# Gathers that fill a bank before copying it, earlier weight loads, and the crowded experts' loop at the end of the expert stage

## The chip, the cores and the metric

One core of one Trainium2 chip runs the kernel in a single launch. The metric is device time in microseconds (us), from one run of the program on the chip; the table below gives the median of three runs and the time of one profiled execution. TensorE (PE) does the matmuls, ScalarE (ACT) and VectorE (DVE) work between PSUM and SBUF, GpSimd (POOL) splits and subtracts in SBUF, and SyncE (SP) issues the DMAs. TensorE's clock is granted by the chip at one of two levels, 2.4 or 1.2 GHz; the profile gives the mean of a stretch as a share of full speed.

## The reference

Two layers, each a mixer (attention and a gated convolution, output matrix `wo`), a mixture of 32 experts (MoE) and a per-layer embedding stage (PLE), on 512 tokens of width 1024. The part that the change touches is the MoE:

```python
# x: 512 tokens x 1024; per layer
n      = rms_norm(x) * nf                 # normalised tokens
p      = softmax(n @ router)              # routing weights over the experts
picks  = the experts chosen for a token, weight g
for e in experts:
    rows = tokens that chose e
    h    = silu(n[rows] @ wg[e]) * (n[rows] @ wu[e])
    x[rows] += g[rows, e] * (h @ wdn[e])
```

Each expert has three weight matrices (`wg`, `wu`, `wdn`) of fp32 numbers, which are read from DRAM once per layer.

## The kernel before

**Pairs of experts.** An expert has room for 64 tokens; two experts form a pair, whose 128 rows fill TensorE's output partitions, 64 each. There are 16 pairs a layer and eight rounds `c` of two pairs. The order of a round on TensorE is written out in `moe`: for each of the two pairs the blocks `g` (the `wg` product) and `u` (the `wu` product), with 32 matmuls each; then `y` (64 matmuls, the `wdn` product of the round before); transposes `hT` of the two pairs; the gather `xg` for the next round (64 matmuls); the combine `c` (32 matmuls) of the round before, which VectorE adds into the tokens (L1079). After the eighth round come the last `y`, a last combine and the PLE stage, whose raw chunks pg0 to pg7 `load_chunks` loads.

**The gather.** Tokens are kept as two parts, `xh` (rounded) and `xl` (the rest). A one-hot matrix picks a pair of pairs' 256 rows. The 1024 columns of a token are worked in eighths k; the two eighths 2h and 2h+1 share one PSUM bank of 512 columns, 256 each, and an eighth is 8 matmuls (four token tiles, two parts). `gather(oh, xg, h)` is called for h = 0 to 3. ScalarE copies each eighth to SBUF (L998). The gather for the first round is made in parts while the tokens are routed (L901, copied by L990), and its last part takes the branch `if self.xg0`.

**Other work of ScalarE in a round.** L1034 starts silu on `g`, L1045 copies the transposes, L1065 scales `y` by the routing weight (`yh`), L1110 rounds the embedding matrix pT that `embeddings` uses in rounds 5 and 6.

**Buffers and queues.** All large tiles (weights, tokens, `xh`, `xl`, `xg`, raw chunks of the other matrices and their split halves) come from 45 slots of 128 x 1024 fp32 (`s4`), handed out in a ring. A weight load is half a matrix row block, 512 KB, and one SP instruction (L241 in `pump`; L253 loads eight late halves of 256 KB). `pump(limit, keep)` issues loads in a fixed order as long as slots are free (keeping `keep` of them) and fewer than `limit` are outstanding. SP issues one DMA at a time in program order, so a load whose slot is not yet free, or whose turn among the eight DMA semaphores has not come, holds all behind it. `RING` gives the limits in the mixer's tail: RING[0] in the eight `ao` steps, RING[1] behind them and in the `wo` steps, RING[2] in the hook that runs while the tokens are routed (`route_tile`, four tiles t).

**Crowded experts.** `overflow` handles experts with more than 64 tokens, in a loop whose count comes from the routing. In this data no expert has that many, so the loop body runs zero times. The loop itself (L1217, L1218) is nevertheless entered: every engine, SP included, comes to its start and waits for all engines and for all DMAs issued so far. Before, it stands in round 4 (`if c == OVC`), behind the combine of pairs 6 and 7.

Of the kernel before, what the change touches and what calls it, by code (L numbers as in the profile page):

```python
# [8 lines left out]
F32 = mybir.dt.float32  # L9
# [3 lines left out]
AF = mybir.ActivationFunctionType  # L13
# [4 lines left out]
T, D, P = 512, 1024, 128  # L18
NT = T // P
# [7 lines left out]
CAP = 64  # L27
GS = 256
# [25 lines left out]
              + [f"wo{i}" for i in range(8)] + ["pe0", "pe1"] + [f"pg{i}" for i in range(8)])  # L54
NCH = len(SEQ_CHUNKS)

RING = 2, 12, 20
KEEP = 6, 10, 6, 6, 8, 10, 12, 8
LAGS = 1, 2, 1, 5
OVC = 4  # L60
PEC = 5
PGD = "pg1", "pg2", "pg3"
PGS = 1, 3, 4, 5, 7
# [18 lines left out]
class Pinned:  # L82


    def __init__(self, tc, e):
        self.tc, self.e = tc, e
# [69 lines left out]
class Trunk:  # L156
    def __init__(self, ctx, tc, x, pT, wd, wg, wu, wdn, sm, gains, cst, out):
        self.tc, self.nc = tc, tc.nc
        self.L = wd.shape[0]
        self.dr = dict(x=x, pT=pT, wd=wd, g=wg, u=wu, d=wdn, sm=sm, gains=gains, cst=cst, out=out)  # L160
        one = ctx.enter_context(tc.tile_pool(name="one", bufs=1))
        rot = ctx.enter_context(tc.tile_pool(name="rot", bufs=1))
        pp = ctx.enter_context(tc.tile_pool(name="ps", bufs=8, space=PSUM))
        self.one, self.tiny = one, ctx.enter_context(tc.tile_pool(name="tiny", bufs=1))
        self.s4 = Slots(rot, "s4", 1024, N4)
        self.s2 = Slots(rot, "s2", 512, N2)
        self.ps = Slots(pp, "ps", 512, 8)
        self.x = [self.s4.get(F32, "x") for _ in range(NT)]
        self.c1 = one.tile([P, C_N1], F32, name="c1")
        self.smt = one.tile([P, S_N], F32, name="smt")  # L170
        self.ident = self.c1[:, C_ID:C_ID + P]
        self.raw, self.hl = {}, {}
        self.loaded = self.split_n = 0
        self.queues, self.adv_n = [], 0

        self.items, self.item_tile, self.item_next, self.ring = [], {}, 0, 0
        for l in range(self.L):
            for c in range(NPAIR // 2 + 1):
                for p in (2 * c, 2 * c + 1) if 2 * c < NPAIR else ():
                    self.items += [(l, w, 2 * p + e, h) for w in ("g", "u") for h in range(4) for e in range(2)  # L180
                                   if p or w == "u" or h < 4 - LATE]
                for p in (2 * c - 2, 2 * c - 1) if c else ():
                    self.items += [(l, "d", 2 * p + e, h) for h in range(4) for e in range(2)]
# [283 lines left out]
    def mixer(self, l):  # L467
        nc = self.nc
        v, act = nc.vector, nc.scalar
# [254 lines left out]
        for j in range(8):  # L724
            c = pos[f"ao{j}"]
            wh, wl = self.take(c)
            pab = [self.ps.get(F32, "ya"), self.ps.get(F32, "yb")]
            for s, src in ((1, cv), (0, oT)):
                for k in range(4):
                    w = slice((4 * s + k) * P, (4 * s + k + 1) * P)  # L730
                    self.mm3(pab[s], wh[:, w], wl[:, w], src[0](k), src[1](k), k == 0, k == 3)
            self.done(c)
            g = gates.pop(0)
            ga, gb = g[:, :T], g[:, T:]
            act.activation(pab[1], pab[1], AF.Identity, bias=self.smt[:, S_BO + j:S_BO + j + 1])
            v.scalar_tensor_tensor(gb, gb, 1.0, pab[1], op0=OP.add, op1=OP.mult)
            v.scalar_tensor_tensor(pab[0], ga, 1.0, pab[0], op0=OP.add, op1=OP.mult)
            v.tensor_tensor(pab[0], pab[0], gb, op=OP.add)
            for h in range(2):
                a = slice(256 * h, 256 * h + 256)  # L740
                act.activation(mT[0].half(j, h), pab[0][:, a], AF.Copy, scale=0.5)
                v.scalar_tensor_tensor(mT[1].half(j, h), pab[0][:, a], 0.5, mT[0].half(j, h).bitcast(F32),
                                       op0=OP.mult, op1=OP.subtract)
            self.ps.free(2)
            self.s4.free()
            self.pump(RING[0])
        for s in oT + tuple(cv):
            s.free()
        self.pump(RING[1])

# [15 lines left out]

        def hook():
            self.advance(steps)
            self.pump(RING[2])
        for t in range(NT):  # L770
            steps.append(self.route_tile(t))
            self.half[t] = self.token_b(cs, mT, t, hook)
# [24 lines left out]
    def route_tile(self, t):  # L797

        nc = self.nc
        v, act, pe = nc.vector, nc.scalar, nc.tensor  # L800
        x, r = self.x[t], self.rc[:, t:t + 1]
# [28 lines left out]
            yield  # L830
        transposes(1)

        hi, lo = self.s4.get(F32R, "xh"), self.s4.get(F32R, "xl")
        act.activation(hi, x, AF.Copy)
        nc.gpsimd.tensor_tensor(lo, x, hi.bitcast(F32), op=OP.subtract)
# [14 lines left out]
        w = self.lgw[:, t * P:(t + 1) * P]  # L850
# [114 lines left out]
    def moe(self, l):  # L965
        nc = self.nc
        self.nc = Engines(self.tc, ("te",))
        v, act, pe = nc.vector, nc.scalar, self.nc.tensor
        oh = self.oh0
# [12 lines left out]
        def gather(oh, xg, h):  # L982

            scale = lambda k: self.smt[:, S_NF + k:S_NF + k + 1]
            out = lambda k: xg[h // 2][:, (k % 4) * GS:(k % 4 + 1) * GS]
            if self.xg0:
                for k in (2 * h, 2 * h + 1):
                    ps = self.xg0.pop(0)[:, :GS]
                    self.gather_part(ps, oh, k, NT - 1)
                    self.last_a = act.activation(out(k), ps, AF.Copy, scale=scale(k)).ins  # L990
                    self.ps.free()
                return
            ps = self.ps.get(F32, "xg")
            for i in range(2):
                k, w = 2 * h + i, slice(i * GS, (i + 1) * GS)
                for t in range(NT):
                    self.gather_part(ps[:, w], oh, k, t)
                act.activation(out(k), ps[:, w], AF.Copy, scale=scale(k))  # L998
            self.ps.free()

        oht, gs, rh, hT, ys = {}, {}, {}, {}, {}
# [118 lines left out]
        NC2 = NPAIR // 2  # L1120
# [5 lines left out]
        for c in range(NC2):  # L1126
            self.c = c
            prs = 2 * c, 2 * c + 1
            if c == PEC - 1:
                load_embeddings()  # L1130
            if c < NC2 - 1:
                oh = self.onehots(c + 1)
            ts = []
            for p in prs:
                pg, pu = self.ps.get(F32, "g"), self.ps.get(F32, "u")
                gate_up(p, xg, "g", pg, range(4))
                gate_up(p, xg, "u", pu, range(4))
                if p == 0:
                    with self.tc.issue_after(self.last_v), self.tc.issue_after(self.last_a):
                        self.route()  # L1140
                        make_rows()
                scatter_hot(p)
                ts.append(hidden(p, pg, pu))
            self.s4.free(2)
            if c == 1:
                restore()
            if c:
                for p in prs:
                    down(p - 2)
            for p, t in zip(prs, ts):  # L1150
                transp(p, t)
            if c < NC2 - 1:
                xg = [self.s4.get(F32, "xg") for _ in range(2)]
                for h in range(4):
                    gather(oh, xg, h)
                self.s4.free()
                if c == NC2 - 2:
                    self.s4.free(2 * NT)
            if c:
                combine((2 * c - 2, 2 * c - 1))  # L1160
            if c == OVC:
                self.overflow(l)
            if c in (PEC, PEC + 1):
                embeddings(c - PEC)
# [5 lines left out]
        pe = nc.tensor  # L1170
# [41 lines left out]
    def overflow(self, l):  # L1212
        nc = self.nc
        v, act, pe, ov = nc.vector, nc.scalar, nc.tensor, self.ov
# [3 lines left out]
        with self.tc.For_i(0, n, 1):  # L1218
            was = self.s4.used, self.s2.used, self.ps.used
            fa, fb, fr = self.s4.get(F32, "ova"), self.s4.get(F32, "ovb"), self.s4.get(F32R, "ovr")  # L1220
            sc, xg, hh, hT, oh, oht = fa[:, :T], fa[:, T:], fb[:, :T], fb[:, T:], fr[:, :T], fr[:, T:]
# [39 lines left out]
            ps = self.ps.get(F32, "ooht")  # L1261
# [5 lines left out]
            for i, q in enumerate((vg, self.rc)):  # L1267
                for t in range(NT):
                    pe.matmul(pg[0:CAP, i:i + 1], oh[:, t * CAP:(t + 1) * CAP].bitcast(F32), q[:, t:t + 1],
                              start=t == 0, stop=t == NT - 1)  # L1270
# [2 lines left out]
            v.tensor_scalar(g[0:CAP], g[0:CAP], rr[0:CAP], None, op0=OP.mult)  # L1273
            self.ps.free()
            px = self.ps.get(F32, "oxg")
            for k in range(KD):
                for t in range(NT):
                    for o in range(2):
                        pe.matmul(px[:, k * CAP:(k + 1) * CAP], self.nh[o][t][:, k * P:(k + 1) * P],
                                  oh[:, t * CAP:(t + 1) * CAP], start=t == 0 and o == 0, stop=t == NT - 1 and o == 1)  # L1280
                act.activation(xg[:, k * CAP:(k + 1) * CAP], px[:, k * CAP:(k + 1) * CAP], AF.Copy,
                               scale=self.smt[:, S_NF + k:S_NF + k + 1])
            self.ps.free()
            pgu = []
            for w in ("g", "u"):
                p_ = self.ps.get(F32, "ogu")
                for h in range(4):
                    wt = weights(w, h)
                    for k in range(2):
                        kk = 2 * h + k  # L1290
                        pe.matmul(p_[0:CAP], xg[:, kk * CAP:(kk + 1) * CAP], wt[:, k * T:(k + 1) * T],
                                  start=kk == 0, stop=kk == KD - 1)
# [13 lines left out]
            for f in range(4):  # L1306
                wt = weights("d", f)
                for n_ in range(2):
                    pe.matmul(py[n_][0:CAP], hT[:, f * CAP:(f + 1) * CAP], wt[:, n_ * T:(n_ + 1) * T],
                              start=f == 0, stop=f == 3)  # L1310
# [172 lines left out]
```

## Time and profile before

| | |
|---|---|
| median of 3 runs | 1946.11 us (1943.98 to 1948.0) |
| profiled execution | 1943.51 us |
| its span, first to last instruction | 1941.7 us, so 1.8 us lie around it |
| mean granted TensorE clock | 0.974 of full |
| TensorE busy | 1812.1 us, 93% |
| DVE, ACT, POOL busy | 916.9, 565.8, 377.9 us |
| DMA queue of SP | 477.04 MB, 65.1% of 16 engines' span |
| MoE of layer 0 | first `g` at 399.7 us, last `y` ends at 916.1 |
| MoE of layer 1 | first `g` at 1360.2 us, last `y` ends at 1871.3 |

A row of the timeline is: start, duration, engine, line of the kernel, operation, output <- inputs, shape, count; in brackets the idle time of the engine just before it and what ended it. Matmuls overlap, so the rate is read from their starts, not from their durations. In a table of stretches "(x8)" is the number of instructions that began there, PEclk the granted clock as a share of full, and the last two columns are the DMA engines' busy share and GB/s. "DVEq", "SPq" stand for an engine's sequencer.

### The profile page before, as it was taken

Reading aid. Unit: us, or ns where it says so; the run is one execution under the profiler, and the core shown is the slowest. Engines: PE = TensorE matmul, PEld = TensorE weight load, DVE = VectorE, ACT = ScalarE, POOL = GpSimd, SP = SyncE. Lnnn points to the kernel's source line nnn. Section 1 sums busy time; section 2 is a strip of 40 time slices with the busy share of each in tenths; the row PEclk is TensorE's granted clock in tenths of the full one; section 3 lists DMA queues with packets and bytes.
Section 4 is the critical chain, followed back from the end, with each engine's and each line's share of the span. In section 5 each row is a group of like instructions: output and inputs, shape, how many; then the busy total and the mean of one; then the engine's idle time right before and its main releaser. Section 6 shows DMA issues by size and latency. Waiting matters only on the chain. (4 is left out here: it accounts for less than half of the span.)

```text
span 1941.7 us, 23302 instructions
## 1 busy us (share of the span) xinstructions
PE 1812.1 (93%) x8532; PEld 1124.4 (58%) x8532; DVE 916.9 (47%) x2165; ACT 565.8 (29%) x1071; POOL 377.9 (19%) x201
## 2 busy tenths in 40 slices
PE   5999999999999889999989999998999989999987
PEld 4776777753454345354767776877444553454456
DVE  5677754652431332323657777537432423332146
ACT  4444444220111012112634555333110111021045
POOL 3444324201000000000444444241010000000021
PEclk9999999999989999999999999999999999999999
DMA  5211227589999889997231112375898989899941
GB/s 217 83 55 66 65 98 227 189 321 357 349 351 410 343 312 382 388 409 303 81 117 65 61 59 66 127 242 195 308 401 326 381 351 401 349 364 409 409 176 44
DMA packets 133319, 478.59 MB, mean 246 GB/s; under 512 B 14800, under 2 KB 15312, under 8 KB 133200
## 3 DMA queue, kind: packets, MB, share of 16 engines
q1 hardware_dynamic: 133200, 477.04, 65.1%
q8 instruction: 70, 1.15, 0.2%
q14 instruction: 49, 0.40, 0.1%
HBM read 474.89 MB, written 2.10 MB: 246 GB/s over the span
## 5 line engine op out<-in xcount | busy, mean ns | idle before, releaser
L230 POOL TENSOR_TENSOR s_lo<-s_raw,s_hi 128x1024 fp32r<-128x1024 f32 x114 | 272.3, 2400 | 950.5 <-ACT s_hi L225 326.6
L94 PE MATMUL ps_g<-s_w,s_xg 128*64 128x512 f32 x1024 | 230.9, 604 | 4.4 <-DVEq L1218 4.4
L94 PE MATMUL ps_y<-s_w,s_hT 128*64 128x512 f32 x1024 | 225.8, 593 | 0.4 <-DMA s_w<-wdn 0.4
L94 PE MATMUL ps_u<-s_w,s_xg 128*64 128x512 f32 x1024 | 225.2, 592 | 0.0
L290 PE MATMUL ps_z<-s_hTl,s_hi 128*128 128x512 f32 x512 | 204.4, 399 | 0.0
L289 PE MATMUL ps_z<-s_hTh,s_hi 128*128 128x512 f32 x512 | 202.0, 395 | 0.0
L291 PE MATMUL ps_z<-s_hTh,s_lo 128*128 128x512 f32 x512 | 200.4, 391 | 0.0
L94 PE MATMUL ps_xg<-s_OH,s_xh 128*128 128x256 f32 x476 | 138.9, 322 | 59.6 <-ACT s_xg L998 55.8
L1079 DVE TENSOR_TENSOR s_x<-s_x,ps_c 128x512 f32<-128x512 f32 x128 | 87.9, 687 | 155.6 <-PE ps_c L94 132.4
L94 PEld LDWEIGHTS ps_y<-s_w,s_hT 128*64 128x64 f32 x1024 | 74.5, 137 | 148.4 <-issue 136.2
L94 PEld LDWEIGHTS ps_g<-s_w,s_xg 128*64 128x64 f32 x1024 | 73.0, 139 | 149.7 <-issue 142.2
L94 PEld LDWEIGHTS ps_u<-s_w,s_xg 128*64 128x64 f32 x1024 | 73.4, 137 | 146.3 <-issue 141.2
L501 DVE SCALAR_TENSOR_TENSOR s_acc<-ps_z,smt,s_acc 128x511 f32<-128x511 f32 (+27 forms) x210 | 153.7, 732 | 4.2
L94 PEld LDWEIGHTS ps_xg<-s_OH,s_xh 128*128 128x128 f32 x476 | 101.4, 213 | 74.2 <-ACT s_xg L998 68.5
L94 PE MATMUL ps_xg<-s_OH,s_xl 128*128 128x256 f32 x476 | 130.9, 305 | 0.0
L225 ACT ACTIVATE s_hi<-s_raw 128x1024 fp32r<-128x1024 f32 x120 | 124.5, 1055 | 0.7
L1034 ACT ACTIVATE s_h<-ps_g,rs 128x512 f32<-128x512 f32 x32 | 22.0, 687 | 343.1 <-PE ps_g L94 331.8
L1035 DVE SCALAR_TENSOR_TENSOR s_h<-s_h,ps_g 128x512 f32<-128x512 f32 x32 | 22.0, 687 | 188.2 <-ACT s_h L1034 188.2
L290 PEld LDWEIGHTS ps_z<-s_hTl,s_hi 128*128 128x128 f32 x512 | 96.7, 189 | 21.4 <-issue 3.0
L289 PEld LDWEIGHTS ps_z<-s_hTh,s_hi 128*128 128x128 f32 x512 | 96.5, 189 | 21.5 <-issue 1.0
L291 PEld LDWEIGHTS ps_z<-s_hTh,s_lo 128*128 128x128 f32 x512 | 96.5, 189 | 19.1
L1045 ACT ACTIVATE s_hT<-ps_hT 128x512 f32<-128x512 f32 x32 | 17.6, 596 | 304.1 <-PE ps_hT L94 263.2
(256 smaller groups left out, 2873.9 us busy)
## 6 DMA issues: line engine op xcount, KB each, us to landing
s_w<-wu SPq DMA_DIRECT2D x256, 512.0 KB, 10.1
s_w<-wdn SPq DMA_DIRECT2D x256, 512.0 KB, 10.2
s_w<-wg SPq DMA_DIRECT2D x248, 512.0 KB, 10.2
s_raw<-wd SPq DMA_DIRECT2D x124, 512.0 KB, 3.5
s_w<-wg SPq DMA_DIRECT2D x16, 256.0 KB, 7.9
s_x<-x SPq DMA_DIRECT2D x4, 512.0 KB, 9.4
out<-s_n SPq DMA_DIRECT2D x8, 256.0 KB, 2.0
s_gain<-gains SPq DMA_DIRECT2D x3, 512.0 KB, 3.7
```

The costliest lines, as they stand in the source:

```text
L94: i = f(*a, **k)
L225: nc.scalar.activation(hi, raw, AF.Copy)
L230: nc.gpsimd.tensor_tensor(lo, raw, hi.bitcast(F32), op=OP.subtract)
L289: mm(out, lh, rh, start=start, stop=False)
L290: mm(out, lh, rl, start=False, stop=False)
L291: mm(out, ll, rh, start=False, stop=stop)
L501: v.scalar_tensor_tensor(o, i, w, o, op0=OP.mult, op1=OP.add)
L1034: act.activation(t, pg, AF.Tanh, scale=rh[p])
L1035: v.scalar_tensor_tensor(t, t, 1.0, pg, op0=OP.add, op1=OP.mult)
L1045: act.activation(o, ps, AF.Copy)
L1079: v.tensor_add(xs, xs, ps)
```

## The change

Five things. `gather` writes both eighths of a bank and only then issues the two copies. `RING` goes from 2, 12, 20 to 6, 18, 28, its first limit grows by one in each `ao` step, and the last pump keeps three slots free. `route_tile` writes each token tile x[t] to a DRAM scratch `xk` before splitting it. The loop of the crowded experts moves from round 4 to the end of round 7, behind the combine of pairs 12 and 13 and ahead of the last `y`. Its body, which runs zero times here, reads the tokens from the scratch.

```diff
-RING = 2, 12, 20
+RING = 6, 18, 28
-OVC = 4
...
-            self.pump(RING[0])
+            self.pump(RING[0] + j)
...
-            self.pump(RING[2])
+            self.pump(RING[2], keep=3)
...
+        if t == 0:
+            self.xkept = [self.dram.tile([P, D], F32, name=f"xk{i}", tag=f"xk{i}") for i in range(NT)]
+        self.nc.sync.dma_start(self.xkept[t], x)
         hi, lo = self.s4.get(F32R, "xh"), self.s4.get(F32R, "xl")
...
             ps = self.ps.get(F32, "xg")
+            half = [ps[:, i * GS:(i + 1) * GS] for i in range(2)]
             for i in range(2):
-                k, w = 2 * h + i, slice(i * GS, (i + 1) * GS)
                 for t in range(NT):
-                    self.gather_part(ps[:, w], oh, k, t)
-                act.activation(out(k), ps[:, w], AF.Copy, scale=scale(k))
+                    self.gather_part(half[i], oh, 2 * h + i, t)
+            for i in range(2):
+                act.activation(out(2 * h + i), half[i], AF.Copy, scale=scale(2 * h + i))
             self.ps.free()
...
-            if c == OVC:
+            if c == NC2 - 1:
                 self.overflow(l)
...
+            xt = []
+            for t in range(NT):
+                xt.append(self.s4.get(F32, "ox"))
+                nc.sync.dma_start(xt[t], self.xkept[t])
```

TensorE's matmuls in the rounds keep their order. On ScalarE, the place is the gather at the end of round 3 (`ps_xg` are its four banks, `pTh` the rounded embedding matrix, L1110 before and L1114 after). Before:

```order
L998 ACTIVATE s_xg_4685<-ps_xg_4687,smt 128x256 x2
L998 ACTIVATE s_xg_4685<-ps_xg_4706,smt 128x256 x2
L998 ACTIVATE s_xg_4686<-ps_xg_4725,smt 128x256 x2
L998 ACTIVATE s_xg_4686<-ps_xg_4744,smt 128x256
L1110 ACTIVATE s_pTh_4811<-s_pT_4813 128x1024
L998 ACTIVATE s_xg_4686<-ps_xg_4744,smt 128x256
```

And after:

```order
L1002 ACTIVATE s_xg_4695<-ps_xg_4697,smt 128x256 x2
L1002 ACTIVATE s_xg_4695<-ps_xg_4716,smt 128x256 x2
L1002 ACTIVATE s_xg_4696<-ps_xg_4735,smt 128x256 x2
L1002 ACTIVATE s_xg_4696<-ps_xg_4754,smt 128x256 x2
L1114 ACTIVATE s_pTh_4821<-s_pT_4823 128x1024
```

The last eighth's copy stood behind the embedding matrix and now stands ahead of it.

On SP, the place is the loop of layer 0 (the branches). Before, round 4, with weight loads on both sides:

```order
L241 DMA s_w_5054<-wu 128x1024
L241 DMA s_w_5060<-wg 128x1024
L241 DMA s_w_5062<-wg 128x1024
L1218 COMPARE_AND_BRANCH
L1218 UNCONDITIONAL_BRANCH x2
```

After, behind the last weight of the layer, with the PLE stage's raw chunks following:

```order
L241 DMA s_w_6292<-wdn 128x1024
L241 DMA s_w_6298<-wdn 128x1024
L1222 COMPARE_AND_BRANCH
L1222 UNCONDITIONAL_BRANCH x2
L1486 BRANCH_PREFETCH_HINT
L1283 DMA s_ox_6475<-xk_2813 128x1024
L1283 DMA s_ox_6477<-xk_2814 128x1024
L1283 DMA s_ox_6479<-xk_2815 128x1024
L1283 DMA s_ox_6481<-xk_2816 128x1024
L1222 REGISTER_ALU
L1222 COMPARE_AND_BRANCH
```

The four scratch reads lie inside the loop. SP comes to the loop with no weight of the layer left to issue.

Also on SP, the end of the mixer of layer 0 after the change, where the fourth token tile (`x_72`) is written to the scratch:

```order
L241 DMA s_w_3105<-wg 128x1024
L241 DMA s_w_3107<-wg 128x1024
L241 DMA s_w_3109<-wg 128x1024
L241 DMA s_w_3111<-wg 128x1024
L835 DMA xk_2816<-s_x_72 128x1024
L253 DMA s_w_3231<-wg 128x512
L253 DMA s_w_3232<-wg 128x512
L253 DMA s_w_3235<-wg 128x512
```

Ten weight loads in a row stand ahead of this write and the late halves behind it; before, the late halves followed the weight loads directly.

## Rows read from the trace of the kernel before

**Rows 1.** The page: the busy time of each engine with its share of the span and its instructions.

```profile
PE 1812.1 (93%) x8532; PEld 1124.4 (58%) x8532; DVE 916.9 (47%) x2165; ACT 565.8 (29%) x1071; POOL 377.9 (19%) x201
```

**Rows 2.** Who waited for whom, on TensorE: total us, times, longest us.

```profile
PE ps_xg L94 <- ACT s_xg L998: 55.8, 58, 2.5
...
PE ps_c L94 <- ACT s_xg L998: 6.3, 2, 4.9
...
PE ps_g L94 <- DVEq L1218: 4.4, 2, 2.2
...
PE ps_wo L290 <- POOL s_lo L230: 0.7, 2, 0.4
...
PE ps_y L94 <- DMA s_w<-wdn: 0.4, 2, 0.2
```

**Rows 3.** Timeline of TensorE in the gather of round 4, layer 0.

```profile
684.86 0.36 PE L94 MATMUL ps_xg<-s_OH,s_xh 128*128 128x256 f32 x1
...
685.77 0.28 PE L94 MATMUL ps_xg<-s_OH,s_xl 128*128 128x256 f32 x1
688.52 0.56 PE L94 MATMUL ps_xg<-s_OH,s_xh 128*128 128x256 f32 x1 [2.46 <-ACT s_xg L998]
...
691.86 0.34 PE L94 MATMUL ps_xg<-s_OH,s_xl 128*128 128x256 f32 x1
692.77 0.38 PE L94 MATMUL ps_xg<-s_OH,s_xh 128*128 128x256 f32 x1 [0.56 <-ACT s_xg L998]
...
694.54 0.28 PE L94 MATMUL ps_xg<-s_OH,s_xh 128*128 128x256 f32 x1
694.66 0.28 PE L94 MATMUL ps_xg<-s_OH,s_xl 128*128 128x256 f32 x1
```

**Rows 4.** Timeline of ScalarE in the same place.

```profile
685.68 2.42 ACT L1065 ACTIVATE s_yh<-ps_y,gs 128x512 fp32r<-128x512 f32 x4
687.95 0.51 ACT L998 ACTIVATE s_xg<-ps_xg,smt 128x256 f32<-128x256 f32 x1
```

**Rows 5.** Table of stretches for the instructions on `ps_xg` alone, one stretch for each of the fourteen whole gathers: stretch, its length, busy us of PE, PEld and ACT, granted clock, DMA share, GB/s. Three of the fourteen (rounds 0, 2 and 5 of layer 0), and the sum over all.

```profile
431.20:442.50 11.30, 8.92 (x64) 7.92 (x64) 3.34 (x8) 1.00 0.87 344
...
547.00:564.00 17.00, 12.72 (x64) 11.46 (x64) 3.37 (x8) 0.70 1.03 409
...
754.70:767.90 13.20, 8.91 (x64) 7.92 (x64) 3.36 (x8) 1.00 1.03 409
...
sum 196.50, PE 140.26 PEld 125.52 ACT 47.06; mean PE 10.02 PEld 8.97 ACT 3.36
```

**Rows 6.** Who SP, which issues the DMAs, waited for, the longest in total: total us, times, longest us.

```profile
SPq L241 <- DMA s_w<-wdn: 213.1, 232, 2.2
```

**Rows 7.** Table of stretches, all engines, in the MoE of both layers: stretch, its length, busy us of the engines, granted clock, DMA share, GB/s.

```profile
400.00:916.00 516.00, 479.35 (x2344) 232.79 (x2340) 165.76 (x361) 74.17 (x136) 16.41 (x7) 0.97 0.93 364
...
400.00:450.00 50.00, 47.42 (x260) 22.44 (x258) 22.29 (x72) 9.68 (x19) 0.00 (x0) 1.00 0.85 315
...
492.00:509.00 17.00, 15.87 (x86) 11.27 (x86) 8.51 (x16) 2.37 (x5) 0.00 (x0) 1.00 0.68 247
...
693.00:714.00 21.00, 17.67 (x88) 12.18 (x89) 10.10 (x22) 2.37 (x5) 0.00 (x0) 0.92 0.52 192
...
787.00:904.00 117.00, 111.08 (x533) 52.69 (x531) 32.20 (x60) 15.61 (x28) 0.00 (x0) 0.99 1.03 409
...
1360.00:1871.00 511.00, 477.61 (x2347) 232.81 (x2345) 166.36 (x360) 74.18 (x136) 16.42 (x7) 0.97 0.94 367
```

**Rows 8.** Timeline of ScalarE, then of TensorE, at the combine of round 3, layer 0.

```profile
637.70 1.06 ACT L1110 ACTIVATE s_pTh<-s_pT 128x1024 fp32r<-128x1024 f32 x1 [11.05 <-DMA s_pT<-pT]
...
639.17 0.79 PE L94 MATMUL ps_c<-s_yh,s_OHT 128*128 128x512 f32 x1 [4.88 <-ACT s_xg L998]
```

**Rows 9.** Timeline of TensorE behind the loop in round 4, layer 0, then the granted clock of that stretch in a table of stretches of TensorE alone.

```profile
708.93 8.78 PE L94 MATMUL ps_g<-s_w,s_xg 128*64 128x512 f32 x32 [2.20 <-DVEq L1218]
717.54 7.04 PE L94 MATMUL ps_u<-s_w,s_xg 128*64 128x512 f32 x32
...
708.00:718.00 10.00, 9.07 (x36) 0.83 0.79 274
```

**Rows 10.** Timeline around the last `y`: SP, ScalarE and TensorE of layer 0, then TensorE of layer 1.

```profile
892.62 9.28 SPq L207 DMA_DIRECT2D s_raw<-wd  x8
...
916.84 1.94 ACT L224 ACTIVATE s_raw<-s_raw,smt 128x512 f32<-128x512 f32 x3
...
902.23 13.95 PE L94 MATMUL ps_y<-s_w,s_hT 128*64 128x512 f32 x64
...
1871.29 0.50 PE L1076 MATMUL ps_c<-s_yh,s_OHT 128*128 128x512 f32 x1
```

**Rows 11.** DMA issues by line: count, KB each, median us from issue to landing.

```profile
s_raw<-wd SPq DMA_DIRECT2D x124, 512.0 KB, 3.5
```

**Rows 12.** Table of stretches, the end of the mixer of layer 0, columns as in rows 7.

```profile
325.00:400.00 75.00, 70.26 (x370) 56.89 (x370) 40.51 (x188) 24.84 (x51) 26.07 (x11) 0.95 0.58 201
```

**Rows 13.** Timeline at the start of the MoE of layer 0: TensorE, ScalarE, TensorE.

```profile
382.94 0.66 PE L807 MATMUL ps_tr<-c,s_x 128*128 128x128 f32 x4 [1.03 <-DVE s_x L827]
...
395.66 2.29 ACT L990 ACTIVATE s_xg<-ps_xg,smt 128x256 f32<-128x256 f32 x6 [8.64 <-PE ps_xg L94]
...
399.71 1.51 PE L94 MATMUL ps_g<-s_w,s_xg 128*64 128x512 f32 x6
```

More of the change, by code (lines that the diff above doesn't have):

```diff
@@ L163, in __init__ @@
         pp = ctx.enter_context(tc.tile_pool(name="ps", bufs=8, space=PSUM))
+        self.dram = ctx.enter_context(tc.tile_pool(name="dram", bufs=1, space=bass.MemoryType.DRAM))
         self.one, self.tiny = one, ctx.enter_context(tc.tile_pool(name="tiny", bufs=1))
@@ L1275, in overflow @@
             px = self.ps.get(F32, "oxg")
+            xt = []
+            for t in range(NT):
+                xt.append(self.s4.get(F32, "ox"))
+                nc.sync.dma_start(xt[t], self.xkept[t])
             for k in range(KD):
                 for t in range(NT):
-                    for o in range(2):
-                        pe.matmul(px[:, k * CAP:(k + 1) * CAP], self.nh[o][t][:, k * P:(k + 1) * P],
-                                  oh[:, t * CAP:(t + 1) * CAP], start=t == 0 and o == 0, stop=t == NT - 1 and o == 1)
+                    pe.matmul(px[:, k * CAP:(k + 1) * CAP], xt[t][:, k * P:(k + 1) * P],
+                              oh[:, t * CAP:(t + 1) * CAP].bitcast(F32), start=t == 0, stop=t == NT - 1)
                 act.activation(xg[:, k * CAP:(k + 1) * CAP], px[:, k * CAP:(k + 1) * CAP], AF.Copy,
```

## The prediction

> **What bounds the kernel now.** I read the page's busy table first, then who waits for whom on TensorE and on the DMA queue, then a table of stretches, and the timeline at the gathers and the loop. TensorE is busy 1812.1 us, 93% of the span [rows 1]: a gain must come out of its waits, its slow-clock stretches, or whatever holds it up next. Its largest wait by far is 55.8 us in 58 pieces, in the gather, on the copy of a half bank; 6.3 us before a combine end on the same copy, 4.4 us on the loop of the crowded experts. On weights it waits 0.4 us in all [rows 2].
>
> The gather at 684.86 shows how. Eight matmuls fill half a bank by 686.05; the next eight go into the other half of that bank, but start at 688.52, after 2.46 us of idling for the copy. ScalarE began that copy at 687.95, since it had the four L1065 instructions (2.42 us) to do first. Each later bank costs another 0.56 us [rows 3, 4]. After the long pause sixteen matmuls take 3.34 us from first to last start, 0.22 us apart, which is 1.2 GHz of granted clock; in the next bank, at 2.4 GHz, they come 0.12 us apart. So 64 matmuls without waits or slow clock take 64 x 0.12 = 7.7 us. The fourteen whole gathers take 196.5 us (windows about 2 us wider than the gathers in all), and in the three shown the granted clock is 1.00, 0.70 and 1.00 of full [rows 5].
>
> The second reading is the DMA queue. On `wdn` loads alone SP waits 213.1 us, in 232 pieces, for an earlier load to land before it may issue the next [rows 6]: in much of the MoE the queue is full. In 787 to 904 it moves 409 GB/s for 117 us, and over the whole MoE of layer 0 364 GB/s [rows 7]. It therefore stands still, in sum, for 516 x (1 - 364/409) = 57 us of 516. **The queue is the next bound, and near.**
>
> **The change part by part.**
>
> *Both eighths, then copies.* The same 64 matmuls and 8 copies; the waits inside a bank go. While TensorE fills one bank, ScalarE copies the bank before: two copies of 0.5 us against 16 x 0.12 = 1.9 us. The first copy still waits for L1065 until 688.1, but TensorE, unhindered, ends its fourth bank only at about 692.5, so the copies keep up. On TensorE alone this gives 196.5 - 2 - 14 x 7.7 = 87 us. At c = 3 the copy of the last eighth also stood behind L1110, which waited 11.05 us for its transfer and held the combine by 4.88 us [rows 8]. In the new order all eight copies come first: 6.3 us more (both layers). What is late next there is L1034's copy of the first pair, needed only when its `h` is transposed, some 40 us later. Sum on TensorE: **93 us**.
>
> *The loop moved.* Its barrier costs 2.20 us, and the following 32 matmuls take 8.78 instead of 7.04 us (clock 0.83 in that stretch): 3.9 us, paid behind c = 4 now and behind c = 7 afterwards. But SP is also held in it: from 693 to 714 the queue moved 192 GB/s, worth 21 x (1 - 192/409) = 11.1 us of stream [rows 7, 9]. That hole goes. In the new place SP has issued every weight of the layer, and the loop makes SP, and with it all engines, wait until **the last weight has landed**, although the last `y` block could have started on its first weights. The eight pg loads queue behind it. Before, they were issued in 892.62 to 901.9 and first read at 916.84 [rows 10]; issued after the loop they still have the 13.95 us of `y`, and a load on a quiet queue takes 3.5 us [rows 11]: 0, at worst about 3 us.
>
> *What the stream allows.* In 400 to 916 the queue moved 516 us x 364 GB/s = 187.8 MB; less the eight pg loads of 0.524 MB, 183.6 MB must land before the loop. At 409 GB/s that is 449 us. To it come holes that remain. Holes before, each as length x (1 - rate/409) from [rows 7]: 11.5 us in 400 to 450 (a full ring, and the first gather), 6.7 at 492 (gather and combine free no slot), 11.1 at the loop; the rest of the 57 lies behind the later gathers and the last load. The first gather becomes 3.5 us shorter (11.2 less 7.7), the second 5.4 (13.1, like the third row shown, less 7.7) [rows 5], which leaves 8 and 1 us of the first two. From then on slots wait for the queue: 48 loads per c at 1.28 us (0.524 MB at 409 GB/s) are 61.5 us, TensorE's own work per c is `y` 13.95, four blocks and a combine of half as many matmuls (5 x 6.95), gather 7.7 and short transposes, together about 57.5. So the later holes vanish. The last weight lands at about 400 + 449 + 9 = 858. Then 2.2 for the loop, 1.7 for slow clock, 13.95 for `y`: the last `y` ends at 876 instead of 916.1 [rows 10], **40 us earlier**. Layer 1 likewise: 511 us x 367 GB/s = 187.5 MB, less 4.2, is 448 us; 1360 + 448 + 9 + 18 = 1835 against 1871.3: **36 us**. This is less than TensorE's 93, so the stream sets the end: 76 us.
>
> *Ring sizes.* They only bring loads forward; the number of free slots when the MoE starts is the same. In 325 to 400 the queue moves 201 GB/s, half of what it can [rows 12], so the loads have room; but the raw chunks of the mixer, 3.5 us from issue to landing [rows 11], now queue with four more weights at first (4 x 1.28 = 5.1 us) and six more later (7.7 us). Chunks are prefetched one ahead and TensorE waits only 0.7 us for a `wo` split in all [rows 2]. From both sides: 0 to 10 us a layer; I take 0, because the queue is half empty there.
>
> *Tokens to DRAM.* Four writes of 0.524 MB a layer at 1.28 us each, 5.1 us of that half-empty queue: 0. The fourth has a price: its source x[3] is the buffer that `xg[1]` takes over, so the copies into it wait for that write. Token tile 3 is final just before its transposes at 382.94; ten weight loads stand ahead of the write and take their slots from about 381.7 on, so it lands at about 381.7 + 11 x 1.28 = 396, or 398 if its issue is late. The six copies of L990 ran from 395.66, the first `g` starts at 399.71 and needs `xg[1]` about 3.4 us later [rows 13]. Bounds 0 to 5 us a layer; I take 0.
>
> *Sum.* 76 us; I keep back 5, chosen, because TensorE's floor (93 us) is only some 8 us a layer away, and where two such bounds lie close each adds small waits to the other. 1943.5 - 71 = **1872.5 us** (1943.5 is the profiled execution, its span and what lies around it). The profiled execution is 0.13% under the median of the runs; I predict 1873 for the median of after.
>
> **The rivals.**
> 1. *The queue hides behind TensorE after all*, for instance because TensorE's rounds are slower than 57.5 us or the ring lasts longer: 1943.5 - 93 = 1850. Against it: 61.5 against 57.5 us per c. Chance 0.15.
> 2. *New waits at the start eat more*: raw chunks 10 us and x[3] 5 us late in each layer, 30 us: 1903. For it: everything is now in one queue. Against: a half-empty queue, one-time delays. Chance 0.12.
> 3. *The other side: a queue that never rests runs slower.* The stream would be unbroken for some 440 us; the longest such stretch so far is 117 us [rows 7]. Layer 0 loses its gain where 183.6 MB need 449 + 40 = 489 us, that is below 375 GB/s; layer 1 below 379. At 360 GB/s the stream takes 61 us longer per layer and the kernel 1943.5 - 71 + 122 = about 1994. No row shows that. Beside this, the Trainium skill's "HBM Reference", section "Specifications (TRN2)", gives about 358 GB/s as a core's effective share; by it there would be no gain at all, and an estimate from it is 183.6/0.358 = 513 us of stream, over 20 us a layer slower than before. The same page says that a core streaming alone measures about 425, and the trace's 409 agrees with that. Chance 0.04.
> 4. *Nothing changes*, because the copies still gate TensorE through the eight banks: 1943. The third bank of a gather takes over the bank of the first `y`, which L1065 reads first of its four, by 686.4, and TensorE reaches it at 688.7. Chance 0.02.
>
> **Numbers.** Forecast 0.67. Predicted 1873. Range 1848 to 1906: it holds the forecast and rivals 1 and 2. No change is anything within 0.2% (4 us), about what a measurement of this kernel can tell. Faster 0.93, same 0.02, slower 0.05.
>
> **What would show it.** TensorE's wait on the half-bank copy almost gone, full gathers near 7.7 us at full clock. In its place waits on weights in the `y` blocks from c = 3 on, several us each, and a long wait of all engines at the loop behind c = 7 (5 to 10 us plus 2.2). MoE of layer 0 near 476 us at about 395 GB/s. Wrong if `y` waits for no weights (rival 1); if `ps_wo` or the first `g` wait for microseconds (rival 2); if full-queue stretches fall under 400 GB/s (rival 3).

## The result and the profile after

The changed kernel takes 1890.33 us (median), against 1945.05 us for the kernel before in the same comparison: a ratio of 0.9719, 95% interval 0.9693 to 0.9745, so 2.8% faster. Predicted were 1873 us and a range of 1848 to 1906. One of the four runs of the changed kernel took 10251 us, for a reason that no record shows; it counts in the median but not in the ratio, and the other three took 1889.2 to 1891.0 us. The profiled execution takes 1889.2 us (before 1943.51), of which the span is 1887.4 us. Of the forecast gain of 71 us, 54 came (profiled executions).

TensorE's row of the busy table, to be laid beside [rows 1], and entries of the view of waits on TensorE, the largest that lie in the MoE or just ahead of it (`ps_xg`), beside [rows 2]:

```profile
PE 1801.5 (95%) x8532; PEld 1108.3 (59%) x8532; DVE 912.3 (48%) x2165; ACT 560.9 (30%) x1071; POOL 377.9 (20%) x201
```

```profile
PE ps_y L93 <- DMA s_w<-wdn: 11.0, 22, 6.8
...
PE ps_y L93 <- DVE ctr L1220: 5.8, 1, 5.8
...
PE ps_u L93 <- DMA s_w<-wu: 3.8, 6, 2.0
PE ps_xg L93 <- DVE s_OH L953: 3.8, 2, 1.9
```

The 55.8 us on the copy of a half bank are gone altogether, and so are the 6.3 us ahead of the combine. New are waits on weights and a wait at the loop, which the view lists under `ctr` in layer 0 and under `wdn` (6.8 us) in layer 1. The gathers, three of layer 0 in the table of stretches for `ps_xg` alone (columns as in [rows 5]), now have the length of their 64 matmuls at full clock:

```profile
478.10:486.00 7.90, 7.81 (x64) 7.74 (x64) 2.55 (x6) 1.00 1.03 408
535.40:543.30 7.90, 7.78 (x64) 7.74 (x64) 2.55 (x6) 1.00 1.03 411
592.80:600.70 7.90, 7.86 (x64) 7.74 (x64) 2.56 (x6) 1.00 1.02 409
```

The table of stretches for all engines in the MoE (columns as in [rows 7]: stretch, length, busy us of PE, PEld, DVE, ACT and POOL, granted clock, DMA share, GB/s):

```profile
396.60:885.00 488.40, 475.76 (x2346) 226.61 (x2345) 165.25 (x369) 72.07 (x139) 16.44 (x7) 0.99 0.98 384
396.60:447.00 50.40, 50.08 (x277) 23.59 (x278) 26.70 (x87) 10.21 (x22) 0.00 (x0) 1.00 0.91 337
...
489.00:506.00 17.00, 17.00 (x80) 7.66 (x80) 12.27 (x30) 0.69 (x1) 0.00 (x0) 1.00 0.94 351
...
608.00:637.00 29.00, 27.04 (x114) 8.75 (x114) 12.18 (x28) 2.32 (x3) 2.37 (x1) 0.94 0.77 293
637.00:740.00 103.00, 100.19 (x480) 49.79 (x478) 30.33 (x61) 16.55 (x32) 4.76 (x2) 1.00 1.03 409
...
850.00:868.00 18.00, 10.77 (x42) 7.66 (x40) 8.23 (x12) 3.40 (x6) 0.00 (x0) 0.88 0.86 341
...
1329.70:1817.00 487.30, 472.79 (x2346) 224.88 (x2345) 165.12 (x368) 72.07 (x139) 16.43 (x7) 0.99 0.98 385
```

The MoE takes 488.4 us in layer 0 (before 516.4, forecast 476) and 487.3 in layer 1 (before 511.1, forecast 475). The queue moves 409 GB/s wherever it is full, as forecast, and rests in few places (8.9 us of stream in the first stretch, 2.4 in 489 to 506). One of them was not forecast: from 608 to 637 it moves only 293 GB/s, which is 29 x (1 - 293/409) = 8.2 us of stream. SP's timeline shows why, and the view of whom SP waited for, in 608 to 624, names it:

```profile
608.94 0.33 SPq L1113 DMA_DIRECT2D s_pT<-pT  x1
622.72 0.80 SPq L207 DMA_DIRECT2D s_raw<-wd  x2
623.62 5.24 SPq L241 DMA_DIRECT2D s_w<-wu  x8
```

```profile
SPq L207 <- DMA s_pT<-pT: 9.8, 1, 9.8
SPq L207 <- POOL s_pTl L1115: 3.6, 1, 3.6
```

SP issues the embedding matrix pT at 608.94 and nothing more until 622.72. The next load, a raw chunk, takes over the slot in which pT is staged; it must wait until pT has landed (9.8 us behind a full queue) and ScalarE and GpSimd have read it (3.6 us). All weight loads stand behind it. The ring runs dry on it at the end of round 4, in the `u` of its second pair and then in `y`:

```profile
630.74 6.89 PE L93 MATMUL ps_u<-s_w,s_xg 128*64 128x512 f32 x18 [1.95 <-DMA s_w<-wu]
...
645.53 2.34 PE L93 MATMUL ps_y<-s_w,s_hT 128*64 128x512 f32 x8 [0.21 <-DMA s_w<-wdn]
648.09 2.35 PE L93 MATMUL ps_y<-s_w,s_hT 128*64 128x512 f32 x8 [0.22 <-DMA s_w<-wdn]
650.65 2.40 PE L93 MATMUL ps_y<-s_w,s_hT 128*64 128x512 f32 x8 [0.21 <-DMA s_w<-wdn]
```

Eight matmuls of `y` now start every 2.56 us, the time of two loads at 1.28; without waits the 64 take 13.95 [rows 10], or 1.74 per eight. This is hard to see in the waits: they list about 0.2 us for each eight, and on `wdn` and `wu` 11.0 + 3.8 - 6.8 (the loop of layer 1) = 8.0 us in all for both layers, though rounds 4 and 5 are 17.9 us longer than without waits in layer 0 alone (worked out below). A matmul's modelled duration hides the rest. The same 64 matmuls, in round 1 and in round 4:

```profile
463.50:477.30 13.80, 13.80 (x66) 4.45 (x62) 2.95 (x3) 0.00 (x0) 2.69 (x2) 1.00 1.03 410
641.80:662.70 20.90, 19.32 (x66) 5.25 (x64) 1.30 (x3) 0.00 (x0) 0.00 (x0) 1.00 1.03 409
```

TensorE is still 92% busy in the second, while the weight loads (PEld) fall from 32% to 25% of the stretch. The Trainium skill, "Perfetto Trace Analysis", section "Identifying the Most-Contended Engine", says that TensorE's matmul busy share is not a good measure of how close it is to roofline, and to use the busy share of LDWEIGHTS (besides the FLOPs done) instead; these rows agree.

Last, the loop, on SP and on TensorE:

```profile
867.82 3.80 SPq L207 DMA_DIRECT2D s_raw<-wd  x8
...
868.31 16.73 PE L93 MATMUL ps_y<-s_w,s_hT 128*64 128x512 f32 x64 [5.79 <-DVE ctr L1220]
```

TensorE stands 5.79 us, and then `y` takes 16.73 instead of 13.95 us, 2.8 more, as it starts at the lower clock; the row of its stretch, 868 to 885, has a granted clock of 0.83:

```profile
868.00:885.00 17.00, 16.69 (x65) 5.17 (x65) 1.61 (x4) 2.06 (x3) 0.00 (x0) 0.83 0.64 248
```

### The profile page after: what moved, and what is told of

It reads as the page before. It is cut to its first block, busy times and chain, and to the rows that moved or that the text cites. A ratio compares the mean times of both kernels' runs of the same rounds, so it can differ in the third digit from the quotient of the medians.

```text
span 1887.4 us, 23302 instructions
## 1 busy us (share of the span) xinstructions
PE 1801.5 (95%) x8532; PEld 1108.3 (59%) x8532; DVE 912.3 (48%) x2165; ACT 560.9 (30%) x1071; POOL 377.9 (20%) x201
## 4 chain that ended last, share of the span: by engine, by line
PE 61%; DMA 23%; DVE 7%; issue 5%; ACT 2%; POOL 1%; SPq 0%; DVEq 0%; POOLq 0%; ACTq 0%
DMA s_w<-wdn 10%; PE ps_g L93 7%; PE ps_u L93 7%; DMA s_w<-wu 7%; PE ps_y L93 6%; PE ps_z L290 5%; PE ps_z L289 5%; PE ps_z L291 5%; PE ps_xg L93 5%; DMA s_w<-wg 4%; PE ps_c L93 2%; PE ps_tb L289 2%; PE ps_tb L290 2%; PE ps_tb L291 2%; PE ps_S L609 2%
## 5 line engine op out<-in xcount | busy, mean ns | idle before, releaser
L93 PE MATMUL ps_y<-s_w,s_hT 128*64 128x512 f32 x1024 | 246.3, 607 | 17.2 <-DMA s_w<-wdn 11.0
L93 PE MATMUL ps_u<-s_w,s_xg 128*64 128x512 f32 x1024 | 232.1, 596 | 5.5 <-DMA s_w<-wu 3.8
L93 PE MATMUL ps_g<-s_w,s_xg 128*64 128x512 f32 x1024 | 226.1, 594 | 0.0
L1083 DVE TENSOR_TENSOR s_x<-s_x,ps_c 128x512 f32<-128x512 f32 x128 | 86.3, 687 | 90.0 <-PE ps_c L93 57.3
L93 PE MATMUL ps_xg<-s_OH,s_xh 128*128 128x256 f32 x476 | 117.4, 288 | 3.8 <-DVE s_OH L953 3.8
L93 PE MATMUL ps_xg<-s_OH,s_xl 128*128 128x256 f32 x476 | 116.0, 285 | 0.0
L93 PEld LDWEIGHTS ps_xg<-s_OH,s_xh 128*128 128x128 f32 x476 | 92.2, 194 | 5.7 <-issue 5.7
## 6 DMA issues: line engine op xcount, KB each, us to landing
s_w<-wu SPq DMA_DIRECT2D x256, 512.0 KB, 10.2
s_w<-wdn SPq DMA_DIRECT2D x256, 512.0 KB, 10.2
s_w<-wg SPq DMA_DIRECT2D x248, 512.0 KB, 10.2
```

The source lines that it names most:

```text
L93: i = f(*a, **k)
L1083: v.tensor_add(xs, xs, ps)
```

## The experiments

Four experiments set a theory on the missing 17 us against rivals. Theory S: the weight stream with its holes sets the end of the MoE. Its rivals: the loop's place matters more (rival L), or less, than that; the waits in round 4 have another cause than pT's slot. From these four runs another theory, T, was formed for four more: TensorE's own chain of work sets the length, and waits on weights and the loop add to it.

**The gather alone.** The kernel before with nothing but the new gather:

```diff
+            half = [ps[:, i * GS:(i + 1) * GS] for i in range(2)]
             for i in range(2):
-                k, w = 2 * h + i, slice(i * GS, (i + 1) * GS)
                 for t in range(NT):
-                    self.gather_part(ps[:, w], oh, k, t)
-                act.activation(out(k), ps[:, w], AF.Copy, scale=scale(k))
+                    self.gather_part(half[i], oh, 2 * h + i, t)
+            for i in range(2):
+                act.activation(out(2 * h + i), half[i], AF.Copy, scale=scale(2 * h + i))
```

> The kernel before with the new gather alone; rings, loop behind round 4 and no scratch as before. Theory S (the weight stream sets the end, at 409 GB/s plus the holes in which SP issues nothing): layer 0 needs 449 us of stream, plus holes of 8.9 and 2.4 at the start, 8.2 where SP stands before the raw chunk behind pT, 11.1 at the loop in round 4, so the last weight lands 480 us after the first g and the last y ends 1 us later; the changed kernel has 488.4, since all engines wait at the loop for the last weight and y follows whole. 8 us a layer less than the changed kernel, 3 us a layer lost again in the mixer: about 1880 us. Rival L (moving the loop to the end is what makes the new gather pay, since its hole in the stream costs 11.1 us a layer and its end place only 5.8): 1889 + 2 x (11.1 - 5.8) + 6 = about 1906 us.

Measured: 1883.61 us, 0.9681 (0.9646 to 0.9717) of before. The one edit gives more than the whole change (its runs took 1881 to 1885 us); rival L falls. TensorE behind the loop in round 4, and the stretch around it:

```profile
687.30 3.68 PE L94 MATMUL ps_g<-s_w,s_xg 128*64 128x512 f32 x8 [5.55 <-DMA s_w<-wg]
```

```profile
672.00:692.00 20.00, 14.45 (x65) 9.61 (x65) 11.32 (x24) 1.68 (x4) 0.00 (x0) 0.83 0.84 320
```

Here the loop costs 5.55 us of idling, not the 2.20 of [rows 9], since loads in flight must land first: SP waits 8.6 us on them at the loop. But its hole in the stream is 20 x (1 - 320/409) = 4.4 us instead of 11.1: SP now comes to the loop at 677.4, 4 us ahead of TensorE; before it came at 692.2, 14 us ahead.

**The loop back behind round 4.** The changed kernel with

```diff
-            if c == NC2 - 1:
+            if c == 4:
                 self.overflow(l)
```

the loop's zero-times body as before, and no scratch writes.

> The changed kernel with the loop back behind round 4 (its body, which runs zero times, reads the split tokens again, and the scratch writes are left out). Theory S: the wait for the last weight and the whole y behind it go, the hole of 11.1 us comes back: MoE about 481 instead of 488 us a layer, 1874 us. Rival L: about 1900 us.

Measured: 1883.09 us, 0.9683 (0.9649 to 0.9717). It equals the gather alone, so the ring sizes, the only difference left, change nothing that these runs can tell; and the move of the loop, together with the scratch writes that came with it, costs the changed kernel 7 us, where rival L had it gain some. Theory S was off by 9.

**No loop.** The changed kernel with the two lines of the loop's call taken out.

> The changed kernel without the loop of the crowded experts (the body runs zero times with this data, so that the numbers are the same, but the kernel would be wrong for other routings). Theory S: no hole and no wait at the end, y ends 1 us behind the last weight, which lands at 449 + 8.9 + 2.4 + 8.2 + 0.7 = 469 us: 18 us a layer less, about 1855 us. Rival (the loop costs only what TensorE idles at it and loses to slow clock behind it, 5.8 + 2.8 us): 8.6 us a layer, about 1872 us.

Measured: 1874.15 us, 0.9638 (0.9604 to 0.9671). The rival's 1872 came within 2 us, and theory S falls here: the last `y` runs whole and unhindered, from its own line in the timeline:

```profile
865.42 13.95 PE L93 MATMUL ps_y<-s_w,s_hT 128*64 128x512 f32 x64
```

It waits for no weight: the last one was issued at 860.7 and landed 10.2 us later, 8.5 us before `y` ends. Round 6, with the embeddings' 24 matmuls beside the rest, lasts 62.8 us, longer than its 48 loads (61.5), so the queue no longer falls behind; at the end of the layer TensorE is last, not the stream. What the stream takes from TensorE, it takes in rounds 4 and 5.

**A buffer of its own for pT.** The changed kernel with

```diff
-N4, N2 = 45, 16
+N4, N2 = 45, 14
...
+        self.praw = one.tile([P, 1024], F32, name="praw")
...
-            praw = self.s4.get(F32, "pT")
+            praw = self.praw
             nc.sync.dma_start(praw, self.dr["pT"][l])
...
-            self.s4.free()
```

> The changed kernel with a buffer of its own for the embedding matrix pT (two of the sixteen small buffers given up for it), so that the raw chunk issued next no longer takes over the slot in which pT is still being read, and SP doesn't stand still before it. Theory S (that standstill, 13.5 us of SP, is the hole of 8.2 us of stream in round 3 or 4 that the forecast let vanish): 8 us a layer less, about 1873 us, the wait on weights in round 4 gone or much smaller. Rival (the wait there comes from the slots kept back, KEEP, or from the stream's rate): no change, 1889 us.

Measured: 1874.92 us, 0.9636 (0.9601 to 0.9671): 15 us less, as expected; the MoE is 9.3 us shorter in layer 0 and 8.4 in layer 1. SP's timeline, and the stretch that holds the place:

```profile
612.82 0.33 SPq L208 DMA_DIRECT2D s_raw<-wd  x1
614.09 0.33 SPq L1114 DMA_DIRECT2D praw<-pT  x1
615.38 0.33 SPq L208 DMA_DIRECT2D s_raw<-wd  x1
616.66 9.28 SPq L242 DMA_DIRECT2D s_w<-wu  x8
```

```profile
602.00:640.00 38.00, 38.00 (x185) 17.69 (x186) 17.45 (x39) 4.01 (x7) 2.40 (x1) 1.00 1.03 409
```

SP goes on at once, the queue stays at 409 GB/s, and `u` in round 4 waits no more; `y` there takes 19.0 instead of 21.1 us. The waits that are left come with the queue full, as the forecast had it: 48 loads take 61.5 us, a round of TensorE 57.3.

```profile
510.00:720.00 210.00, 208.26 (x1027) 95.74 (x1024) 65.25 (x140) 25.75 (x50) 2.40 (x1) 1.00 1.03 409
```

**Theory T.** In the changed kernel a round without waits takes 57.3 us, 62.8 with the embeddings; with round 0 (39.4), round 7 up to its combine (53.8) and the last `y` (13.95), TensorE's own chain is 39.4 + 4 x 57.3 + 2 x 62.8 + 53.8 + 13.95 = 462 us. What each kernel's layer 0 has above that, from the starts of its rounds in the timeline:

| kernel | waits on weights, rounds 4 and 5 | loop: idle + slow clock behind it | sum | MoE of layer 0 measured |
|---|---|---|---|---|
| after | 17.9 | 5.8 + 2.8 | 488.5 | 488.4 |
| gather alone | 14.5 | 5.6 + 2.4 | 484.5 | 484.9 |
| loop in round 4 | 13.7 | 5.9 + 2.4 | 484.0 | 484.4 |
| no loop | 18.0 | 0 | 480.0 | 480.5 |
| pT buffer | 9.1 | 5.2 + 2.0 | 478.3 | 479.1 |
| loop last | 9.0 | 0 | 471.0 | 471.5 |
| loop in round 2 | 6.1 | 7.3 + 2.2 | 477.6 | 478.0 |

The first column is the length of rounds 4 and 5 less 57.3 and 62.8 and, where the loop stands in them, less the loop. Sum and measurement come from the same timeline, so their agreement shows only that nothing large is left out; what the rows compare is the kernels.

With a loop in round 4 or ahead of it the waits on weights are 3 to 4 us smaller (14.5 and 13.7 for 18.0, 6.1 for 9.1), so it stands in for part of them, presumably since loads land while TensorE pauses; at the end of round 7 it comes on top.

**The loop behind the last y**, with the pT buffer:

```diff
-            if c == NC2 - 1:
-                self.overflow(l)
...
         down(NPAIR - 2)
         down(NPAIR - 1)
+        self.overflow(l)
```

> The changed kernel with the buffer of its own for pT, and the loop behind the last y instead of ahead of it; the pg chunks are issued ahead of the loop. Theory T (TensorE's own chain needs 462 us a layer; added to it are the waits on weights in rounds 3 and 4, which come from holes in the stream, and at the loop the wait for the last weight plus slow clock): the 5.2 us of waiting and 2.0 us of slow clock at the last y of the kernel with the pT buffer go, a barrier of 2.2 us and up to 2 us for the last copies come instead: 3 to 4 us a layer less, 1867 to 1869 us. Rival (the pg chunks then land behind the loop, and the barrier waits for them as it did for the last weight): no gain or 1 to 2 us a layer more, 1875 to 1879 us.

Measured: 1864.02 us, 0.9585 (0.9555 to 0.9615), the fastest of all: 26 us under the changed kernel, though it keeps the loop. The direction is theory T's, the rival falls; but the gain over the kernel with the pT buffer is 10.9 us, where 6 to 8 were expected. Against the kernel with the pT buffer the MoE is 7.7 and 9.4 us shorter in the two layers. Behind `y` the barrier takes a part back; TensorE now idles 5.36 us there:

```profile
856.13 13.95 PE L93 MATMUL ps_y<-s_w,s_hT 128*64 128x512 f32 x64
875.44 0.80 PE L1081 MATMUL ps_c<-s_yh,s_OHT 128*128 128x512 f32 x1 [5.36 <-ACT s_hi L226]
```

The stretches behind the two layers' last `y` are 3.0 and 2.9 us longer, and the first `g` comes 1.7 us earlier: 7.7 + 9.4 - 3.0 - 2.9 + 1.7 = 12.9 us, the whole difference of the two spans (1874.4 and 1861.5).

**The loop behind round 2**, with the pT buffer, the body as before and no scratch writes:

```diff
-            if c == NC2 - 1:
+            if c == 2:
                 self.overflow(l)
```

> The changed kernel with the buffer of its own for pT, and the loop behind round 2, where the ring is still nearly full (its zero-times body reads the split tokens, no scratch writes). Theory T: a hole in the stream costs the same wherever it lies ahead of rounds 3 and 4, since the ring runs dry there: 462 + 9 + 11 + 4 = 486 us a layer, 1887 us. Rival (a full ring hides SP's standstill in round 2): 462 + 9 + 4 = 475 us, 1867 us.

Measured: 1870.57 us, 0.9617 (0.9586 to 0.9647). The stretch of the loop and TensorE behind it:

```profile
546.00:568.00 22.00, 14.69 (x58) 7.89 (x58) 12.37 (x28) 0.66 (x2) 0.00 (x0) 0.84 0.81 293
...
560.36 1.97 PE L93 MATMUL ps_g<-s_w,s_xg 128*64 128x512 f32 x4 [7.31 <-DVE s_OH L951]
```

Neither theory's reason is right. The full ring hides nothing: TensorE stands 7.31 us, while SP waits 9.1 us at the loop for what is in flight. But the hole is 22 x (1 - 293/409) = 6.2 us, not the 11 taken from [rows 7], and rounds 4 and 5 wait 6.1 instead of 9.1 us; that the ring loses nothing in TensorE's pause would explain it, but is not shown by itself.

**The old gather in the changed kernel**, the first experiment's diff the other way round:

> The changed kernel with the old gather (half a bank, copy, half a bank, copy); rings, scratch and the loop at the end stay. Theory T: TensorE's waits in the gather leave the queue enough rest, so nothing but the place of the loop and the mixer change: 0 to 4 us a layer less than before, 1936 to 1945 us. Rival (the earlier loads or the loop's place carry part of the gain by themselves): under 1930 us.

Measured: 1945.95 us, 0.9999 (0.9976 to 1.0021). Rings, scratch and the loop's place by themselves change nothing beyond that interval (about 4 us either way); what is gained comes through the gather. The waits on TensorE are the old ones:

```profile
PE ps_xg L93 <- ACT s_xg L1001: 55.8, 58, 2.5
```

**No loop and no scratch.** The kernel without the loop, less `self.nc.sync.dma_start(self.xkept[t], x)`:

> The kernel without the loop, and without the eight writes of the tokens to DRAM, which nothing reads then. If the scratch writes cost nothing, the same as the kernel without the loop alone, 1874 us within 2; if the fourth write holds up the first copies of xg, 2 to 6 us less.

Measured: 1872.74 us, 0.9631 (0.9600 to 0.9662), against 1874.15 with the writes. The intervals overlap almost whole: the writes cost at most 2 us or so. The gather alone with pT's own buffer was not run, nor was pT's own buffer without any loop.

## Why the prediction came out as it did

**Right: what bounds next.** TensorE's gain of 93 us could not be kept, because the weight stream and TensorE are close. The full queue moves 409 GB/s in every stretch, however long; rival 3 (a queue that slows down when it never rests) is refuted: 103 us at 409 in the profile after, and 210 us at 409 with pT's own buffer. The Trainium skill's figure of about 425 GB/s for a core alone ("HBM Reference", "Specifications (TRN2)") goes with that, its 358, the share of each core when both cores of a domain stream, does not apply to this run of one core.

**Right: the gather.** 7.9 us at full clock, no wait left; forecast 7.7. That ScalarE copies all eight before pT also took away the 6.3 us.

**Right: the price of the new place of the loop.** All engines wait there for the last weight. Forecast were 5 to 10 us of waiting plus 2.2; there are 5.8 in all (6.8 in layer 1), below that, and 2.8 of slow clock where 1.7 were taken.

**Wrong: "So the later holes vanish."** The step compared 48 loads of 1.28 us with TensorE's round and let every hole after the second go. But a faster TensorE does away only with those holes in which SP stands still for want of a slot that TensorE has yet to free. In round 4 SP stands for another reason, the slot of pT, for 13.5 us, and a faster TensorE does not shorten that. The hole was there before the change, behind the wait of 11.05 us in [rows 8], which the prediction read as a wait of ScalarE alone. In the trace before, SP issues pT at 627.61 and nothing more until 641.23, with the same two waits, and the stretch loses 20 x (1 - 245/409) = 8.0 us of stream:

```profile
627.61 0.33 SPq L1109 DMA_DIRECT2D s_pT<-pT  x1
641.23 0.80 SPq L207 DMA_DIRECT2D s_raw<-wd  x2
```

```profile
SPq L207 <- DMA s_pT<-pT: 9.7, 1, 9.7
...
SPq L207 <- POOL s_pTl L1111: 3.6, 1, 3.6
```

```profile
630.00:650.00 20.00, 15.12 (x57) 7.21 (x58) 11.30 (x23) 1.59 (x3) 2.36 (x1) 0.83 0.66 245
```

The prediction counted it in "the rest of the 57", behind the later gathers. Its price: 8.2 us a layer by the stream, 15 us in all by the run with pT's own buffer. The other holes came out at 8.9 and 2.4 us for 8 and 1; the holes behind the later gathers did go (6.9 us in 561 to 580 before; 547 to 564, the same gather, moves 408 GB/s after).

**The account.** Forecast were 458 us from the first `g` to the last weight; now the stream takes 449 + 8.9 + 2.4 + 8.2, together with small rests 470 (the queue runs empty between 864 and 867). These 12 us are those by which the MoE is longer than forecast (488.4 for 476; layer 1, 487.3 for 475). The first `g` of layer 0 comes 3 us earlier, where 0 were taken, and about half a microsecond is lost elsewhere: 76 - 24 + 2.4 = 54. The 3 us are luck as far as the runs tell: in the experiments with the new rings the first `g` comes between 397.7 and 400.3, with the old rings at 399.7. The 5 us kept back covered a fifth of the 24.

**Right, but only by way of the loop: the stream sets the end.** In the changed kernel TensorE reaches the loop at 862.5 and stands until 868.3, and the last weight lands in that time; so the stream does set the start of the last `y`, as forecast. It is not the bound by itself: TensorE comes there 17.9 us late from rounds 4 and 5, and without the loop the last `y` ends 8.5 us behind the last weight and the kernel is 19 us above the estimate that takes the stream as the end's bound. The forecast's waits of "several us each" in `y` belong to the same loss, but its sum has no term for them. With the loop it needs none, since TensorE waits there for the last weight anyway; without the loop they are what makes TensorE late.

**The terms at nothing.** Rings and the scratch were taken at 0 with bounds of 10 and 5 us a layer: the loop in round 4 equals the gather alone (1883.1 and 1883.6 us), and the writes cost at most 2 us or so in the whole kernel. The waits on weights came in `u` and `y` of round 4 and `y` of round 5, one round later than forecast. Rival 2 didn't come.

## What to carry to other kernels

When two resources run close, list every stretch in which the second one rests, and name for each what its issuing engine waits for: here the rests for want of free buffers behind the later gathers went away when TensorE sped up, and the rest with another reason stayed (8.0 us before, 8.2 after) and was then paid for. A staging buffer whose slot the very next load takes over stops the whole queue for a landing plus its readers, here 9.8 + 3.6 us. Of the three places tried for the barrier with pT's own buffer, the cheapest lies behind the last use of the weights (1864 us, against 1871 in round 2 and 1875 ahead of the last `y`). And take a change apart: the new gather alone, an edit of seven lines, gave about 60 us where the whole change gave 55.

## What the runs showed that was not expected

A loop that runs zero times costs TensorE 2.2 us of idling where the queue has run empty before TensorE comes to it [rows 9], and 5.6, 5.9 and 7.3 us where loads are still in flight. The hole that it leaves in the stream was larger where SP came there further ahead of TensorE: 11.1 us before, with SP 14 us ahead, and 4.4 and 6.2 us in the experiments, with SP 4 us ahead.
